# Gate and up of two FFNs by seven block products instead of eight

## The chip, the cores and the metric

The kernel runs on one core of a Trainium2 chip (trn2). Its time is the device time of one execution in microseconds (us). In the profile the engines are PE (TensorE, with PEld for its weight loads), DVE (VectorE), ACT (ScalarE), POOL (GpSimd) and SP (SyncE, which here only issues transfers). Each engine works off its own instructions in a fixed order; one that has to wait holds up all behind it on that engine.

## The reference

A diffusion backbone of two layers over 256 latent and 256 context tokens with 1024 features, all in float32. Each layer is a half FFN, a token mixer (grouped Fourier mixing in layer 0, bidirectional retention in layer 1), and a second half FFN:

```python
def half_ffn(t, m, j):
    h = modulate(rmsnorm(t, norm_g[l, j]), m[3 * j], m[3 * j + 1])
    return t + 0.5 * m[3 * j + 2] * swiglu(h, ffn_w_gate[l, j // 2], ffn_w_up[l, j // 2], ffn_w_down[l, j // 2])
def swiglu(h, w_gate, w_up, w_down):
    return (jax.nn.silu(h @ w_gate) * (h @ w_up)) @ w_down
```

The inner width is 2816. Both streams, latent and context, go through the same weights; only the last half FFN runs on the latent stream alone. The modulation vectors `m` (nine per layer, 1024 long, one set for each stream) come from products of a conditioning vector with 75 MB of weights.

## The kernel before

Activations lie transposed: features on the 128 partitions, in 8 tiles ("d tiles"), tokens in columns 0..255 (latent) and 256..511 (context). The four FFNs are called FFN 0 to 3 here (`f` in the code).

**Precision.** Float32 is reached by splitting each operand into two float32r parts, `hi` and `lo` (`split`: a cast on ScalarE for `hi`, a subtraction on VectorE for `lo`), and three matmuls for each product: hi x hi, hi x lo, lo x hi (`mm3`, lines 121 to 123 of the profile). So all weights pass through ScalarE (L88, tile `wh`) and VectorE (L89, tile `wl`) in tiles of 128 x 1024, after a transfer into `raw` (L95, queue of SP). `wpool` holds 5 such pairs, `rpool` 3 raw tiles of 2048 columns.

**An FFN** (`half_ffn`). The inner width is 22 tiles of 128 ("f tiles"), done in three chunks (`CHUNKS`: 8, 7, 7). For an f tile, gate and up are two PSUM tiles of 128 x 512 (both streams), each the sum over 8 d tiles of three matmuls: 48 matmuls of 512 columns, with two weight tiles of 1024 columns. `hidden` then makes silu(gate) on ScalarE (L383), the product with up on VectorE (L385), and its split, into `a` tiles. After each chunk the down projection adds into the residual (`residual`, L331); in the last chunk `project_last` finishes the latent half first, so that the norm of the next sublayer (`prepare`, `norm_mod`, L325 to L327) runs beside the context half.

**The head of FFN 1 and 2** (`begin_two`): two f tiles are done for the latent stream first, in matmuls of 256 columns, then the context's norm (`late`) and their context half. Their weights' `lo` parts are made on POOL.

**Modulation vectors** are worked ahead on VectorE (`pump`, `ada_step`, L211): a step is one d tile of one vector, for both streams, and reads 512 KB through POOL's queue (L202, two buffers `araw`). `pump(1.5)` follows each f tile and each of the four blocks of the down projection in FFN 1 and 2, with a credit for the halves, until all 128 steps are done.

**Order.** The program is written with a tile framework whose scheduler orders the instructions of each engine at build time; `tc.issue_after(x)` keeps a group behind instruction x.

Of the kernel before, what the change touches and what calls it, by code (L numbers as in the profile page):

```python
# [35 lines left out]
def hybrid_block(ctx: ExitStack, tc: tile.TileContext, a: dict, out: bass.AP):  # L36
    nc = tc.nc
    const = ctx.enter_context(tc.tile_pool(name="const", bufs=1))
    hpool = ctx.enter_context(tc.tile_pool(name="hpool", bufs=16))
# [57 lines left out]

    def wblock(src, n, other=None, lo_eng=None):
        """Loads up to 2048 columns, as pairs of parts that add up exactly, in tiles of 1024."""
        raw = load_raw(src, n)  # L100
        if other is not None:
            two = load_raw(other, n)
            for i, op in enumerate((ALU.add, ALU.subtract)):
                u, v = (t.rearrange("p (g f c) -> p g f c", f=2, c=256)[:, :, i] for t in (raw, two))
                nc.gpsimd.tensor_tensor(u, u, v, op)
# [988 lines left out]
```

## Time and profile before

| what | value |
|---|---|
| time, median of 3 runs (lowest, highest) | 1686.03 us (1685.74, 1686.68) |
| span of the profiled execution | 1685.4 us |
| busy: PE, DVE, ACT, POOL | 97%, 68%, 37%, 10% of the span |
| matmuls; instructions on DVE | 9384; 1769 |
| read from HBM | 261.08 MB, 156 GB/s over the span |
| share of the chain that ended last | PE 91%, DVE 5%, DMA 2%, ACT 1% |

The span is the time from the first to the last instruction of one profiled execution; the timed runs lie some 0.6 us above it. A duration in the profile is that of one instruction from start to end. Instructions of one engine overlap a little at their ends, so what an engine needs for a row of them is read from start to start in the timeline. A window (`A:B`) gives the busy time of each engine between two times, and the clock that TensorE was granted (PEclk, 1.00 is full).

### The profile page before, as it was taken

To read this page: it belongs to the slowest core of one execution; us is meant where nothing else is said; L and a number is where in the kernel's file an instruction comes from. 1 tells how busy PE (TensorE), PEld (TensorE's weight loads), DVE (VectorE), ACT (ScalarE), POOL (GpSimd) and SP (SyncE) were. 2 spreads that over 40 slices of the span, in tenths; PEclk is the share of its full clock that TensorE was granted. 3 is DMA by queue.
4 is the path that set the end of the run, shared out by engine and by line. 5 is a ranking of instruction groups with operands and counts; after the bars stand their busy time and mean duration, and the time that the engine had idled before them with its cause. 6 is when DMAs were issued, how large, how long until landed. Compare 5 with 4: busy or idle time off the path is not lost.

```text
span 1685.4 us, 23227 instructions
## 1 busy us (share of the span) xinstructions
PE 1637.7 (97%) x9384; PEld 1432.7 (85%) x9384; DVE 1142.5 (68%) x1769; ACT 624.0 (37%) x904; POOL 176.1 (10%) x213
## 2 busy tenths in 40 slices
PE   6999999997999999999999999999999999999998
PEld 4788888886888888888888888888998989999998
DVE  5678788768876766766567766743577657575554
ACT  4522322244452223223343132223465354454444
POOL 0011011035210000000400000000400000110000
PEclk9999999998999999999999999999999999999999
DMA  9555555554224554554234444522233324345452
GB/s 334 211 189 200 193 185 209 190 175 150 89 88 150 175 175 161 177 172 165 104 124 164 172 159 166 178 103 94 76 125 125 126 101 150 125 165 180 169 194 69
DMA packets 52892, 263.63 MB, mean 156 GB/s; under 512 B 6321, under 2 KB 7729, under 8 KB 34609
## 3 DMA queue, kind: packets, MB, share of 16 engines
q1 hardware_dynamic: 33664, 193.46, 32.7%
q0 software_dynamic: 18576, 68.17, 12.0%
q8 instruction: 73, 1.20, 0.3%
q10 hardware_dynamic: 544, 0.52, 0.1%
q14 instruction: 35, 0.28, 0.0%
HBM read 261.08 MB, written 1.05 MB: 156 GB/s over the span
## 4 chain that ended last, share of the span: by engine, by line
PE 91%; DVE 5%; DMA 2%; ACT 1%; issue 1%; SPq 0%; DVEq 0%; ACTq 0%
PE ps L122 30%; PE ps L121 30%; PE ps L123 30%; DMA a<-in_ada_first 1%; DVE q L325 1%; DVE h L327 1%; ACT wh L88 1%; DVE wl L89 1%; DVE q L286 0%; DMA xctx<-in_x 0%; PE ps L702 0%; DMA raw<-in_wgu 0%; DVE xctx L331 0%; PE aux L239 0%; DVE q L267 0%
## 5 line engine op out<-in xcount | busy, mean ns | idle before, releaser
L88 ACT CAST wh<-raw 128x1024 fp32r<-128x1024 f32 x344 | 353.2, 1030 | 714.7 <-PE ps L122 665.4
L122 PE MATMUL ps<-h,wh 128*128 128x512 f32 (+1 forms) x1600 | 564.2, 354 | 5.2 <-DVE h L327 5.2
L123 PE MATMUL ps<-h,wl 128*128 128x512 f32 (+1 forms) x1600 | 562.3, 354 | 0.0
L121 PE MATMUL ps<-h,wh 128*128 128x512 f32 (+1 forms) x1600 | 556.5, 355 | 3.7 <-ACT h L88 2.7
L89 DVE TENSOR_TENSOR wl<-raw,wh 128x1024 fp32r<-128x1024 f32 x328 | 392.6, 1199 | 172.6 <-ACT wh L88 163.6
L122 PEld LDWEIGHTS ps<-h,wh 128*128 128x128 f32 x1600 | 303.0, 189 | 48.2 <-DVE h L327 6.7
L121 PEld LDWEIGHTS ps<-h,wh 128*128 128x128 f32 x1600 | 299.4, 190 | 46.0 <-ACT h L88 3.5
L123 PEld LDWEIGHTS ps<-h,wl 128*128 128x128 f32 x1600 | 302.8, 189 | 41.2
L211 DVE CUSTOM_DVE_ANT_0 dump<-araw,wide,adab 128x1024 bf16<-128x1024 f32 x256 | 329.4, 1287 | 3.8
L122 PE MATMUL ps<-a,wh 128*128 128x256 f32 (+2 forms) x980 | 324.1, 332 | 0.0
L123 PE MATMUL ps<-a,wl 128*128 128x256 f32 (+2 forms) x980 | 323.6, 331 | 0.0
L121 PE MATMUL ps<-a,wh 128*128 128x256 f32 (+2 forms) x980 | 322.0, 331 | 0.0
L122 PEld LDWEIGHTS ps<-a,wh 128*128 128x128 f32 x980 | 186.1, 190 | 17.6
L123 PEld LDWEIGHTS ps<-a,wl 128*128 128x128 f32 x980 | 186.1, 190 | 17.4
L121 PEld LDWEIGHTS ps<-a,wh 128*128 128x128 f32 x980 | 185.2, 190 | 17.5
L385 DVE TENSOR_TENSOR t<-ps,t 128x512 f32<-128x512 f32 (+1 forms) x88 | 55.0, 625 | 189.9 <-PE ps L123 182.8
L202 POOL DMA_DIRECT2D araw<-in_ada_w x128 | 67.7, 529 | 809.4 <-DVE mods L211 742.4
L331 DVE SCALAR_TENSOR_TENSOR xlat<-ps,mods,xlat 128x256 f32<-128x256 f32 x128 | 61.1, 481 | 72.0 <-PE ps L123 71.4
L383 ACT ACTIVATE t<-ps 128x512 f32<-128x512 f32 (+1 forms) x88 | 47.9, 545 | 133.2 <-PE ps L123 133.2
L89 DVE TENSOR_TENSOR a<-t,a 128x512 fp32r<-128x512 f32 (+2 forms) x116 | 73.4, 637 | 3.9 <-ACT a L88 3.6
L89 POOL TENSOR_TENSOR wl<-raw,wh 128x1024 fp32r<-128x1024 f32 x16 | 40.1, 2522 | 312.3 <-ACT wh L88 312.3
L88 ACT CAST a<-t 128x512 fp32r<-128x512 f32 (+2 forms) x116 | 64.2, 557 | 9.2 <-DVE t L731 7.4
(189 smaller groups left out, 1200.9 us busy)
## 6 DMA issues: line engine op xcount, KB each, us to landing
raw<-in_wgu SPq DMA_DIRECT2D x85, 1024.0 KB, 5.0
araw<-in_ada_w POOLq DMA_DIRECT2D x128, 512.0 KB, 3.7
raw<-in_wd SPq DMA_DIRECT2D x32, 896.0 KB, 5.8
raw<-in_ret_in SPq DMA_DIRECT2D x24, 1024.0 KB, 4.8
raw<-in_wd SPq DMA_DIRECT2D x16, 1024.0 KB, 6.3
a<-in_ada_first SPq DMA_DIRECT2D x32, 256.0 KB, 5.2
raw<-in_four_w SPq DMA_DIRECT2D x8, 1024.0 KB, 4.8
raw<-in_ret_out SPq DMA_DIRECT2D x8, 1024.0 KB, 4.7
```

The source lines that it names most:

```text
L88: nc.scalar.copy(hi, src)
L89: i = (lo_eng or nc.vector).tensor_tensor(lo, src, f32(hi), ALU.subtract)
L121: nc.tensor.matmul(ps, lh, rh, start=start, stop=False)
L122: nc.tensor.matmul(ps, lh, rl, start=False, stop=False)
L123: mark[4] = nc.tensor.matmul(ps, ll, rh, start=False, stop=stop)
L202: nc.gpsimd.dma_start(raw, a["ada_w"][l, m, d])
L211: nc.vector.tensor_tensor_reduce(dump, raw, wide[:, v, :], 1.0, adab[:, l, m, d : d + 1], ALU.mult, ALU.add, mods[l][:, m, d, v : v + 1],)
L325: nc.vector.scalar_tensor_tensor(u, x_tile(d, s), sc, r, ALU.mult, ALU.mult)
L327: done.append(nc.vector.scalar_tensor_tensor(lo, u, sh, f32(hi), ALU.add, ALU.subtract))
L331: mark[0] = nc.vector.scalar_tensor_tensor(x_tile(d, s), ps, mods[l][:, m, d, s : s + 1], x_tile(d, s), ALU.mult, ALU.add)
L383: mark[1] = nc.scalar.activation(sg[:, :width], psg[:, :width], AF.Silu)
L385: nc.vector.tensor_tensor(hf[:, :width], psu[:, :width], sg[:, :width], ALU.mult)
```

## The change

For FFN 1 and FFN 2 the f tiles are taken in 11 pairs, and a pair's gate and up are computed by Strassen's method in Winograd's form: a block matrix product with blocks A11, A12 (first f tile, halves of d), A21, A22 (second f tile) and B11, B21 (latent stream, halves of d), B12, B22 (context stream). Seven products of blocks take the place of eight. Each product is 4 d tiles x gate and up x 3 matmuls of 256 columns, 24 in all, into one PSUM tile.

- **Activations** (`norm_blocks`, once per FFN): beside B11, B21 and B22 four blocks T1 to T4 of sums and differences of the streams' halves, each cast and split; 28 `h` tiles instead of 16.
- **Weights** (`pair_weights`, per pair): four sums S1 to S4 of 128 x 1024, made in place on the raw tiles by VectorE (L440 of the new file), and seven tiles to cast and split (L88 there) instead of four.
- **Results** (`pair_steps`): products accumulate in three PSUM tiles per pair; three are copied out by ScalarE (`kept`), three sums are made on VectorE (L495, L510, L517), and silu and the product with up go in four pieces of 256 columns (L478, L476).
- **Head** (`run_pairs`): two pairs are interleaved; their products with the latent stream come first, then the context's norm, then the rest. `begin_two`, and the `lo` parts on POOL with it, are no longer used by FFN 1 and 2. `pump` is called twice for the two pairs of the head, and twice for each pair after them.
- **Room**: chunks of 8, 8, 6 f tiles in all FFNs; raw tiles of 1024 columns (7 of them, so twice as many transfers of half the size); 4 weight pairs instead of 5; 18 `a` tiles instead of 22; some tiles of the Fourier mixing, retention and the first modulation move to `h` tiles; the scratch of POOL's transfers is set to 4096 bytes.

```diff
-CHUNKS = ((0, 8), (8, 15), (15, 22))
+CHUNKS = ((0, 8), (8, 16), (16, 22))
...
-    hpool = ctx.enter_context(tc.tile_pool(name="hpool", bufs=16))
-    apool = ctx.enter_context(tc.tile_pool(name="apool", bufs=22))
-    tpool = ctx.enter_context(tc.tile_pool(name="tpool", bufs=6))
+    hpool = ctx.enter_context(tc.tile_pool(name="hpool", bufs=28))
+    apool = ctx.enter_context(tc.tile_pool(name="apool", bufs=18))
+    tpool = ctx.enter_context(tc.tile_pool(name="tpool", bufs=8))
...
-    mpool = ctx.enter_context(tc.tile_pool(name="mpool", bufs=2))
-    rpool = ctx.enter_context(tc.tile_pool(name="rpool", bufs=3))
-    wpool = ctx.enter_context(tc.tile_pool(name="wpool", bufs=5))
+    rpool = ctx.enter_context(tc.tile_pool(name="rpool", bufs=7))
+    wpool = ctx.enter_context(tc.tile_pool(name="wpool", bufs=4))
...
     def load_raw(src, n):
-        raw = rpool.tile([P, 2048], F32, tag="raw", name=nm("raw"))
-        nc.sync.dma_start(raw[:, :n], src)
+        raw = []
+        for o in range(0, n, WT):
+            m = min(WT, n - o)
+            raw.append(rpool.tile([P, WT], F32, tag="raw", name=nm("raw")))
+            nc.sync.dma_start(raw[-1][:, :m], src[:, o : o + m])
         return raw
...
+    def blocks_of_h():
+        return {b: [(h_tile(), h_tile()) for _ in range(2)] for b in ("B11", "B21", "T1", "T2", "T3", "B22", "T4")}
+    def norm_blocks(l, j, s, H, r, V):
+        last = []
+        def values(i):
+            v = a_tile(F32)
+            with tc.issue_after(last[-2].ins) if len(last) > 1 else nullcontext():
+                for o in range(2):
+                    d = 2 * i + o
+                    u = q_tile()
+                    sc, sh = mods[l][:, 3 * j + 1, d, s : s + 1], mods[l][:, 3 * j, d, s : s + 1]
+                    nc.vector.scalar_tensor_tensor(u, x_tile(d, s), sc, r, ALU.mult, ALU.mult)
+                    nc.scalar.activation(v[:, o * S : o * S + S], u, AF.Identity, bias=sh)
+            return v
+        def parts(b, i, v):
+            hi, lo = H[b][i]
+            nc.scalar.copy(hi, v)
+            last.append(nc.vector.tensor_tensor(lo, v, f32(hi), ALU.subtract))
+        if s == 0:
+            for i in range(4):
+                V[i] = values(i)
+                parts(("B11", "B21")[i // 2], i % 2, V[i])
+        else:
+            n1, n2, v12, v22 = [], [], [], []
+            for i in range(2):
+                v12.append(values(i))
+                n1.append(t_tile())
+                nc.vector.tensor_tensor(n1[i], V[i], v12[i], ALU.subtract)
+                parts("T1", i, n1[i])
+            for i in range(2):
+                v22.append(values(2 + i))
+                n2.append(t_tile())
+                nc.vector.scalar_tensor_tensor(n2[i], n1[i], -1.0, v22[i], ALU.mult, ALU.subtract)
+                parts("T2", i, n2[i])
...
+            for i in range(2):
+                t = t_tile()
+                nc.vector.scalar_tensor_tensor(t, n2[i], -1.0, V[2 + i], ALU.mult, ALU.subtract)
+                parts("T4", i, t)
+        mark[0] = last[-1]
+    def pair_weights(f, p):
+        a11, a12 = load_raw(a["wgu"][f, 2 * p], 2048)
+        a21, a22 = load_raw(a["wgu"][f, 2 * p + 1], 2048)
+        at = {"A11": a11, "A12": a12, "A22": a22, "S1": a21, "S2": a11, "S3": a11, "S4": a12}
+        sums = [("S1", a21, a22, ALU.add), ("S2", a11, a21, ALU.add), ("S4", a12, a11, ALU.add), ("S3", a11, a22, ALU.subtract)]
+        def block(b):
+            while any(o == b for o, *_ in sums):
+                _, u, v, op = sums.pop(0)
+                nc.vector.tensor_tensor(u, u, v, op)
+            hi = wpool.tile([P, WT], F32R, tag="wh", name=nm("wh"))
+            lo = wpool.tile([P, WT], F32R, tag="wl", name=nm("wl"))
+            split(hi, lo, at[b])
+            return hi, lo
+        return block
+    def pair_steps(f, p, H, hid):
+        block = pair_weights(f, p)
+        al, be, ga = (ps_tile() for _ in range(3))
+        made, keep = {}, {}
+        def product(ps, w, b, first, ks=range(4)):
+            if 0 in ks:
+                made[w] = block(w)
+            wh, wl = made[w]
+            for k in ks:
+                hi, lo = (t[:, k % 2 * S : k % 2 * S + S] for t in H[b][k // 2])
+                for gu in range(2):
+                    o = gu * 512 + k * P
+                    for i, (u, v) in enumerate(((wh, hi), (wh, lo), (wl, hi))):
+                        mark[4] = nc.tensor.matmul(
+                            ps[:, gu * S : gu * S + S], u[:, o : o + P], v, start=(first and k + gu + i == 0),
+                            stop=(k == 3 and i == 2), skip_group_check=True,
+                        )
+        def kept(n, ps):
+            keep[n] = t_tile()
+            nc.scalar.copy(keep[n], ps)
+        def silu_mult(c, dst, sign=1.0):
+            g = q_tile()
+            mark[1] = nc.scalar.activation(g, c[:, :S], AF.Silu, scale=sign)
+            if sign < 0:
+                nc.vector.scalar_tensor_tensor(dst, c[:, S:], sign, g, ALU.mult, ALU.mult)
+            else:
+                nc.vector.tensor_tensor(dst, c[:, S:], g, ALU.mult)
+        at = len(hid)
+        hid += [(a_tile(), a_tile()) for _ in range(2)]
+        def out(n):
+            split(*hid[at + n], keep[n])
+        def p1(ks=range(4)):
+            product(al, "A11", "B11", True, ks)
+            if 3 in ks:
+                kept("p1", al)
+        def p2(ks=range(4)):
+            product(be, "A12", "B21", True, ks)
+            if 3 in ks:
+                c = t_tile()
+                nc.vector.tensor_tensor(c, be, keep["p1"], ALU.add)
+                keep[0] = t_tile()
+                silu_mult(c, keep[0][:, :S])
+        def p5():
+            product(ga, "S1", "T1", True)
+            kept("p5", ga)
+        def p6():
+            product(al, "S2", "T2", False)
+            kept("u2", al)
+        def p7():
+            product(al, "S3", "T3", False)
+            c = t_tile()
+            nc.vector.scalar_tensor_tensor(c, al, -1.0, keep["p5"], ALU.mult, ALU.subtract)
+            keep[1] = t_tile()
+            silu_mult(c, keep[1][:, S:])
...
+        def p4():
+            product(al, "A22", "T4", False)
+            silu_mult(al, keep[1][:, :S], -1.0)
+            out(1)
+        return p1, p2, p5, p6, p7, p3, p4
...
+            if paired:
+                run_pairs(f, h, hid, c0 // 2, c1 // 2)
+                i = c1
+            elif c0 == 0:
...
+    def prepare(l, j, width, paired=False):
...
+                norm = (lambda s, r: norm_blocks(l, j, s, h, r, V)) if paired else (lambda s, r: norm_mod(l, j, s, h, r))
+                norm(0, rstd(0))
...
+    def run_pairs(f, H, hid, p0, p1):
+        if p0 == 0:
+            two = [pair_steps(f, p, H, hid) for p in range(2)]
+            for n in range(2):
+                for ks in ((0, 1), (2, 3)):
+                    for steps in two:
+                        steps[n](ks)
+                if n == 0:
+                    nxt["late"](0)
+            nxt["late"](1)
+            for n in range(2, 7):
+                for steps in two:
+                    steps[n]()
+                if n == 4:
+                    pump(RATE[f])
+            pump(RATE[f])
+            p0 = 2
+        for p in range(p0, p1):
+            s1, s2, s5, s6, s7, s3, s4 = pair_steps(f, p, H, hid)
+            for n, step in enumerate((s1, s2, s6, s5, s7, s3, s4)):
+                step()
+                if n == 4:
+                    pump(RATE[f])
+            pump(RATE[f])
...
-    fourier(0, 0, nxt["h"], late, prepare(0, 2, T2))
-    half_ffn(0, 2, nxt["h"], T2, begin_two, prepare(1, 0, T2))
+    fourier(0, 0, nxt["h"], late, prepare(0, 2, T2, True))
+    half_ffn(0, 2, nxt["h"], T2, begin_two, prepare(1, 0, T2, True))
...
-    nc = bacc.Bacc("TRN2", target_bir_lowering=False, num_devices=1)
+    nc = bacc.Bacc("TRN2", target_bir_lowering=False, num_devices=1, dynamic_dma_scratch_size=4096)
```

Three places show how the instructions stand before and after. In all of them `xctx` is the context's residual, `raw` a weight tile as loaded, `wh` and `wl` its parts, `h` an activation's parts, `ps` a PSUM tile, `dump` a half step of the modulation vectors.

VectorE at the head of FFN 1, before: the context's norm begins (reciprocal, then one scaling and one `lo` part per d tile).

```order
L286 RECIPROCAL q_872_4229<-q_871_4227 128x256
L325 SCALAR_TENSOR_TENSOR q_873_4282<-xctx_1_94,mods0_123,q_872_4229 128x256
L325 SCALAR_TENSOR_TENSOR q_874_4286<-xctx_1_94,mods0_123,q_872_4229 128x256
L325 SCALAR_TENSOR_TENSOR q_875_4290<-xctx_1_94,mods0_123,q_872_4229 128x256
L327 SCALAR_TENSOR_TENSOR h_823_4077<-q_873_4282,mods0_123,h_822_4076 128x256
L325 SCALAR_TENSOR_TENSOR q_876_4294<-xctx_1_94,mods0_123,q_872_4229 128x256
L327 SCALAR_TENSOR_TENSOR h_825_4079<-q_874_4286,mods0_123,h_824_4078 128x256
```

VectorE there, after; `raw_924` to `raw_927` are the second pair's weights, `ps_918` and `ps_929` hold the second products of the two pairs.

```order
L440 TENSOR_TENSOR raw_926_4264<-raw_926_4264,raw_927_4266 128x1024
L495 TENSOR_TENSOR t_948_4385<-ps_918_4254,t_939_4319 128x512
L440 TENSOR_TENSOR raw_924_4260<-raw_924_4260,raw_926_4264 128x1024
L88 TENSOR_TENSOR wl_978_4506<-raw_926_4264,wh_977_4505 128x1024
L440 TENSOR_TENSOR raw_925_4262<-raw_925_4262,raw_924_4260 128x1024
L88 TENSOR_TENSOR wl_981_4537<-raw_913_4245,wh_980_4536 128x1024
L478 TENSOR_TENSOR t_949_4387<-t_948_4385,q_950_4388 128x256
L495 TENSOR_TENSOR t_951_4403<-ps_929_4269,t_940_4333 128x512
L88 TENSOR_TENSOR wl_984_4568<-raw_924_4260,wh_983_4567 128x1024
L440 TENSOR_TENSOR raw_913_4245<-raw_913_4245,raw_916_4251 128x1024
L393 SCALAR_TENSOR_TENSOR q_955_4410<-xctx_1_91,mods0_120,q_943_4339 128x256
```

The reciprocal and the context's scalings stood together; now these weight sums, weight splits and two sums out of PSUM stand between them.

TensorE at the same place, before: the end of the latent half of the second f tile, then the context half (`h_822` is the first d tile's `hi` part).

```order
L121 MATMUL ps_864_4169<-h_836_4090,wh_868_4176 128x256
L122 MATMUL ps_864_4169<-h_837_4091,wh_868_4176 128x256
L123 MATMUL ps_864_4169<-h_836_4090,wl_869_4177 128x256
L121 MATMUL ps_861_4166<-h_822_4076,wh_857_4158 128x256
L121 MATMUL ps_862_4167<-h_822_4076,wh_857_4158 128x256
L121 MATMUL ps_863_4168<-h_822_4076,wh_866_4172 128x256
```

TensorE there, after: the end of the second pair's product with B21, then S1 times T1 (`h_871` and `h_872` are the `hi` and `lo` part of T1's first two d tiles; `ps_919` belongs to the first pair, `ps_930` to the second).

```order
L463 MATMUL ps_929_4269<-h_869_4155,wh_946_4357 128x256
L463 MATMUL ps_929_4269<-h_870_4156,wh_946_4357 128x256
L463 MATMUL ps_929_4269<-h_869_4155,wl_947_4358 128x256
L463 MATMUL ps_919_4255<-h_871_4157,wh_974_4474 128x256
L463 MATMUL ps_930_4270<-h_871_4157,wh_977_4505 128x256
L463 MATMUL ps_919_4255<-h_872_4158,wh_974_4474 128x256
```

What follows the latent products now reads T1, a difference of latent and context values, and S1, a sum of weights; before it read the context's normalised values themselves.

VectorE in the middle of FFN 1, before: from one f tile's product of gate and up to the next one's.

```order
L385 TENSOR_TENSOR t_959_4797<-ps_957_4746,t_958_4795 128x512
L89 TENSOR_TENSOR wl_994_4962<-raw_992_4959,wh_993_4961 128x1024
L89 TENSOR_TENSOR a_961_4800<-t_959_4797,a_960_4799 128x512
L211 ISA dump_962_4803,mods1_124<-araw_947_4727,wide_122,adab_107 128x1024
L211 ISA mods1_124 128x1
L211 ISA dump_963_4805,mods1_124<-araw_947_4727,wide_122,adab_107 128x1024
L211 ISA mods1_124 128x1
L89 TENSOR_TENSOR wl_996_4966<-raw_992_4959,wh_995_4965 128x1024
L385 TENSOR_TENSOR t_973_4871<-ps_971_4820,t_972_4869 128x512
```

VectorE in the middle of the second chunk of FFN 1, after: from the split of one pair's S3 (`raw_1253`) to the sum that follows its product; `raw_1299` to `raw_1302` belong to the next pair.

```order
L88 TENSOR_TENSOR wl_1279_6321<-raw_1253_6177,wh_1278_6320 128x1024
L214 ISA dump_1247_6165,mods1_121<-araw_1206_5912,wide_119,adab_104 128x1024
L214 ISA mods1_121 128x1
L88 TENSOR_TENSOR wl_1287_6361<-raw_1254_6179,wh_1286_6360 128x1024
L88 TENSOR_TENSOR wl_1291_6396<-raw_1256_6183,wh_1290_6395 128x1024
L88 TENSOR_TENSOR wl_1311_6456<-raw_1299_6440,wh_1310_6455 128x1024
L214 ISA dump_1248_6167,mods1_121<-araw_1206_5912,wide_119,adab_104 128x1024
L214 ISA mods1_121 128x1
L440 TENSOR_TENSOR raw_1299_6440<-raw_1299_6440,raw_1301_6444 128x1024
L510 SCALAR_TENSOR_TENSOR t_1280_6348<-ps_1257_6185,t_1277_6316 128x512
L214 ISA dump_1250_6171,mods1_121<-araw_1239_6095,wide_119,adab_104 128x1024
L214 ISA mods1_121 128x1
```

Two weight splits and a step stood between two results out of PSUM; now, between S3's split and the sum behind its product, stand three more weight splits, a weight sum and a step.

More of the change, by code (lines that the diff above doesn't have):

```diff
@@ L78, in a_tile, with h_tile @@
         return apool.tile([P, 512], dt, tag="a", name=nm("a"))
-    def h_tile():
-        return hpool.tile([P, 512], F32R, tag="h", name=nm("h"))
+    def h_tile(dt=F32R):
+        return hpool.tile([P, 512], dt, tag="h", name=nm("h"))
     def f32(ap):
@@ L101, in wblock @@
         if other is not None:
[L102 to L105, printed above, removed]
+            for pair in zip(raw, load_raw(other, n)):
+                for i, op in enumerate((ALU.add, ALU.subtract)):
+                    u, v = (t.rearrange("p (g f c) -> p g f c", f=2, c=256)[:, :, i] for t in pair)
+                    nc.gpsimd.tensor_tensor(u, u, v, op)
         pairs = []
-        for o in range(0, n, WT):
+        for o, t in zip(range(0, n, WT), raw):
             m = min(WT, n - o)
@@ L110, in wblock @@
             lo = wpool.tile([P, WT], F32R, tag="wl", name=nm("wl"))
-            split(hi[:, :m], lo[:, :m], raw[:, o : o + m], lo_eng)
+            split(hi[:, :m], lo[:, :m], t[:, :m], lo_eng)
             pairs.append((hi, lo))
@@ L372, in project_last @@
         after(1)
+    def blocks_of_h():
[34 more added lines that the diff above has]
+                t = t_tile()
+                nc.vector.tensor_tensor(t, v22[i], v12[i], ALU.subtract)
+                parts("T3", i, t)
+            for i in range(2):
+                parts("B22", i, v22[i])
+            for i in range(2):
+                t = t_tile()
+                nc.vector.scalar_tensor_tensor(t, n2[i], -1.0, V[2 + i], ALU.mult, ALU.subtract)
+                parts("T4", i, t)
+        mark[0] = last[-1]
@@ new lines, in pair_steps, with p3 @@
+    def pair_steps(f, p, H, hid):
[52 more added lines that the diff above has]
+            silu_mult(c, keep[1][:, S:])
+        def p3():
+            product(ga, "S4", "B22", False)
+            c = t_tile()
+            nc.vector.tensor_tensor(c, ga, keep["u2"], ALU.add)
+            silu_mult(c, keep[0][:, S:])
+            out(0)
+        def p4():
[3 more added lines that the diff above has]
+        return p1, p2, p5, p6, p7, p3, p4
@@ L375, in half_ffn @@
     def half_ffn(l, j, h, width, begin, after, each=None):
+        paired = isinstance(h, dict)
         f = 2 * l + j // 2
@@ L444, in fourier @@
         raw = load_raw(a["dft"][:, :1280], 1280)
-        dft = [(a_tile(), a_tile()) for _ in range(2)]
+        dft = [(h_tile(), h_tile()) for _ in range(2)]
         for i, (hi, lo) in enumerate(dft):
-            split(hi, lo, raw[:, 512 * i : 512 * i + 512], nc.gpsimd)
+            split(hi, lo, raw[0][:, 512 * i : 512 * i + 512], nc.gpsimd)
         fix = a_tile()[0:33, :S]
-        nc.scalar.copy(fix, raw[0:33, 1024:1280])
+        nc.scalar.copy(fix, raw[1][0:33, :256])
         def dcols(o):
             return tuple(t[:, o % 512 : o % 512 + S] for t in dft[o // 512])
-        tails = mpool.tile([P, 512], F32, tag="mk", name="tails")
+        tails = h_tile(F32)
         nc.sync.dma_start(tails, a["dft"][:, 1280:1792])
@@ L461, in fourier @@
         nc.scalar.mul(edge, ident[:64].unsqueeze(1).broadcast_to([64, 2, P]), 0.0)
-        even = [(a_tile(), a_tile()) for _ in range(4)]
+        even = [(a_tile(), h_tile()) for _ in range(4)]
         odd = [(a_tile(), a_tile()) for _ in range(2)]
@@ L619, in masks @@
             nc.vector.scalar_tensor_tensor(m2, delta, 0.0, e2, ALU.is_le, ALU.mult)
-            own = mpool.tile([P, 512], F32, tag="mk", name=nm("mk"))
+            own = h_tile(F32)
             nc.vector.tensor_tensor(own, m1, m2, ALU.add)
@@ L869, in late @@
                     else:
-                        norm_mod(l, j, 1, h, nxt["r"])
+                        norm(1, nxt["r"])
                 nxt["late"] = late
```

16 lines of the change are left out of this document (7 added, 9 removed).

## The prediction

> **What bounds the kernel now.** I read the page's busy line and the chain of waits first, then windows over FFN 1 and FFN 2, then the timeline of TensorE and VectorE inside them.
>
> ```profile
> PE 1637.7 (97%) x9384; PEld 1432.7 (85%) x9384; DVE 1142.5 (68%) x1769; ACT 624.0 (37%) x904; POOL 176.1 (10%) x213
> ...
> PE 91%; DVE 5%; DMA 2%; ACT 1%; issue 1%; SPq 0%; DVEq 0%; ACTq 0%
> ```
>
> TensorE is the bound nearly everywhere: 97% busy, 91% of the chain. The two changed FFNs begin with the scalings of their latent norm and the reciprocal before them:
>
> ```profile
> 471.91 1.26 DVE L325 SCALAR_TENSOR_TENSOR q<-xlat,mods,aux 128x256 f32<-128x256 f32 x3 [2.21 <-PE aux L311]
> ...
> 831.98 1.75 DVE L286 RECIPROCAL q<-q 128x256 f32<-128x256 f32 x1 [2.37 <-ACT q L283]
> ...
> 1196.95 1.75 DVE L286 RECIPROCAL q<-q 128x256 f32<-128x256 f32 x1 [2.37 <-ACT q L283]
> ```
>
> So FFN 1 takes 472 to 832, 360 us, and FFN 2 takes 832 to 1197, 365 us. Windows over both (columns: PE, PEld, DVE, ACT, POOL busy with counts, clock, DMA share, GB/s):
>
> ```profile
> 472.00:832.00 360.00, 359.57 (x1738) 304.50 (x1738) 243.01 (x359) 109.18 (x146) 37.04 (x58) 1.00 0.45 155
> 832.00:1197.00 365.00, 363.36 (x1771) 307.66 (x1770) 226.01 (x323) 111.73 (x151) 36.99 (x49) 1.00 0.41 140
> ```
>
> TensorE never stops there. VectorE has 117 and 139 us left, and the question is whether the new sums fit. Prices per instruction, read from start to start:
>
> ```profile
> 540.25 0.39 PE L121 MATMUL ps<-h,wh 128*128 128x512 f32 x1
> ...
> 558.61 0.39 PE L121 MATMUL ps<-h,wh 128*128 128x512 f32 x1
> ...
> 483.91 0.28 PE L121 MATMUL ps<-h,wh 128*128 128x256 f32 x1
> ...
> 484.63 0.28 PE L121 MATMUL ps<-h,wh 128*128 128x256 f32 x1
> ...
> 542.72 1.23 DVE L89 TENSOR_TENSOR wl<-raw,wh 128x1024 fp32r<-128x1024 f32 x1
> 543.86 0.68 DVE L89 TENSOR_TENSOR a<-t,a 128x512 fp32r<-128x512 f32 x1
> 544.46 1.28 DVE L211 CUSTOM_DVE_ANT_0 dump<-araw,wide,adab 128x1024 bf16<-128x1024 f32 x1
> ...
> 547.12 1.28 DVE L211 CUSTOM_DVE_ANT_0 dump<-araw,wide,adab 128x1024 bf16<-128x1024 f32 x1
> ...
> 447.48 0.41 DVE L551 TENSOR_TENSOR t<-ps,t 128x256 f32<-128x256 f32 x1
> 447.81 0.41 DVE L552 TENSOR_TENSOR t<-ps,t 128x256 f32<-128x256 f32 x1
> 448.14 0.47 DVE L331 SCALAR_TENSOR_TENSOR xlat<-t,mods,xlat 128x256 f32<-128x256 f32 x1
> 448.53 0.47 DVE L331 SCALAR_TENSOR_TENSOR xctx<-t,mods,xctx 128x256 f32<-128x256 f32 x1
> ```
>
> Between the first two rows lie 81 matmuls: 18.36 / 81 = 0.227 us for 512 columns. Between the next two lie 6: 0.72 / 6 = 0.120 us for 256, more than half. On VectorE 1024 columns cost 1.14, 512 cost 0.60, 256 cost 0.33 or, with a scalar operand, 0.40, and a modulation step (two halves, 544.46 to 547.12) 2.66 us. To see that such prices add up, I multiplied them with the instructions that FFN 1 and 2 had before: 240 and 217 us. The windows show 243 and 226 busy, the rest being stretched instructions at the heads (below).
>
> **TensorE's part of the change.** A pair before is 96 matmuls of 512 columns, 96 x 0.227 = 21.8 us; after, 168 of 256, 168 x 0.120 = 20.2. The two f tiles of the head were in 256 columns already, 192 x 0.120 = 23.0. Per FFN: 23.0 + 10 x 21.8 = 240.7 before, 11 x 20.2 = 221.8 after, so 18.9 less, 37.8 for both. That is all the change can gain on TensorE. The smaller last chunk changes nothing worth counting.
>
> **VectorE's part.** A pair before: 4 weight splits (4.6), two products of gate and up and their splits (4 x 0.60 = 2.4), three modulation steps (8.0), together 15.0 beside 21.8 of TensorE. After: 7 weight splits and 4 weight sums (11 x 1.14 = 12.5), three sums out of PSUM and two splits (3.0), four products of 256 (1.5), the same three steps (8.0), together 25.0 beside 20.2. The in-place sum has no row before; I price it as the split, the same operation on the same sizes. It could be as dear as a half step (1.33) or, from below, nothing dearer than the 0.60 of 512 columns if some faster form applied: 43 sums in an FFN then shift it by +8 or -23 us of VectorE time; no row shows a faster form, so 1.14. With 14 splits and 8 sums of activations (512 columns) in each norm, in place of 16 `lo` parts, VectorE needs 361 us for FFN 1 and 335 for FFN 2 by all its instructions. FFN 1 alone thus fills VectorE for as long as the whole of it takes now. FFN 2 is lighter since the 128 steps run out in it.
>
> What counts is where it lies. While gate and up run, VectorE needs 22 to 24 us from one pair to the next by the new order (two to four steps moved into the down projection), over TensorE's 20.2; in the down projections TensorE needs more. Stage by stage, the larger of the two, FFN 1 first.
>
> *Head, to the second block of the third pair.* Two waits, both for rooms and data that the first weights hold:
>
> ```profile
> L88 ACT CAST wh<-raw 128x1024 fp32r<-128x1024 f32 x344 | 353.2, 1030 | 714.7 <-PE ps L122 665.4
> ...
> raw<-in_wgu SPq DMA_DIRECT2D x85, 1024.0 KB, 5.0
> ```
>
> The fifth weight tile (S1) needs a `wpool` buffer from the first product: about 7 us after the first scaling, plus a cast of 1.03 and a split, 9.2. The eighth raw tile of the two pairs needs the buffer that this split frees (seven buffers), so it lands at 14.2 (5.0 from issue; half the size may take less). Behind it on VectorE stand four weight sums, three splits and two sums out of PSUM (9.5), and only then the context's scalings, and T1 (4.9): T1 is there at 28.6. TensorE had four products, 11.5 us from 2.7 on, and waits from 14.2 to 28.8. Then 12 products, 34.6, and 2.5 for a clock that has dropped by then: 66 us. VectorE's own sum ends at 64. Before, the same wait was nothing.
>
> ```profile
> 398.00:404.00 6.00, 3.26 (x13) 2.89 (x14) 5.94 (x14) 3.84 (x10) 2.66 (x3) 0.58 0.50 175
> 404.00:410.00 6.00, 6.00 (x27) 5.02 (x27) 5.97 (x10) 3.28 (x9) 4.04 (x3) 0.57 0.17 41
> ...
> 838.00:842.00 4.00, 3.13 (x24) 2.92 (x24) 4.00 (x6) 1.74 (x5) 2.68 (x1) 1.00 0.04 14
> ```
>
> After a real stop (398 to 404) the clock stood near half for some 5 us, half of which is the 2.5; with TensorE idle in crumbs (838 to 842, 78% busy) it stayed at 1.00. [...]
>
> *The rest of FFN 1.* Pairs 3 and 4: VectorE 45.5; its last 4 (the tail of the last result) lie beside the next stage, 41.5. Down projection, 192 x 0.227 = 43.5, with two products of the next pair, 5.8: 49.3 on TensorE (VectorE 41.8). Four pairs of chunk 2: 90.8 - 4 = 86.8 on VectorE (TensorE 74.9). Down: 49.3. Three pairs: 65.9 - 4 = 61.9 (TensorE 54.7). Last down to the next reciprocal: 72 x 0.227 + 72 x 0.120 = 25, and 2 for the norm's sum and root. Together 66 + 41.5 + 49.3 + 86.8 + 49.3 + 61.9 + 27 = 382, against 360: +22.
>
> *FFN 2* begins at its reciprocal, so its head is 72; then 38.8, 49.3, 87.4, 49.3; with no steps left the last three pairs are TensorE's, 54.7, and 27: 378.5 against 365, +13.5.
>
> *POOL's splits go.* They had stretched VectorE's instructions:
>
> ```profile
> 838.58 2.68 POOL L89 TENSOR_TENSOR wl<-raw,wh 128x1024 fp32r<-128x1024 f32 x1 [2.24 <-ACT wh L88]
> ...
> 833.96 3.46 DVE L325 SCALAR_TENSOR_TENSOR q<-xlat,mods,q 128x256 f32<-128x256 f32 x3
> ...
> 838.92 2.62 DVE L325 SCALAR_TENSOR_TENSOR q<-xlat,mods,q 128x256 f32<-128x256 f32 x1
> ```
>
> Three scalings took 3.46 instead of 1.3 and one 2.62 instead of 0.48, some 4.3 us in FFN 2's head. Since the stages above use undisturbed prices, this gain is in them. [...]
>
> *The rest.* Seven weight splits and sums (8.0) move into the end of the Fourier mixing, where VectorE is on the chain; they fill gaps and what POOL no longer takes: +2 (0 to 8). ScalarE per pair: seven casts, three copies, silu and casts, some 11 us of 22: hidden by VectorE's queue, and if it is late VectorE waits; with SP's and POOL's transfers I put all waits inside VectorE's stretches (455 us) at 2%, +8 (0 to 20), as 404 to 410 shows VectorE at 5.97 of 6 when it is the bound. Twice as many transfers on SP's queue, fewer weight and `a` buffers elsewhere, and POOL's smaller scratch cost 0 as long as ScalarE's casts wait for TensorE (665 of 715 us of their idle time, above); if that cover goes in retention or FFN 3, a few us. I take 0 (0 to +6).
>
> Sum: 1685.4 + 22 + 13.5 + 2 + 8 = 1731, on the profiled execution's span, which lies 0.6 below the median of the runs; that changes nothing at this size.
>
> **Rivals.** (a) *Slower modulation.* TensorE sets the time after all, since steps yield: without them VectorE needs 17 us per pair, under 20.2. It decides where fewer than 1.2 steps stand between two pairs; the order has two to three, and VectorE cannot pass over them. If it held, and the heads' stops with it (2 x 12), the time is 1686 - 38 + 24 = 1672; without those stops 1648. [...] (c) *Balance*: VectorE runs ahead in the down projections so far that the stops of both FFNs cost no more than the 38 saved, 1686. The four weight buffers hold less than one pair, so hardly. (d) *The products don't get cheaper*: with weight loads of 190 ns not overlapped, 168 x 0.19 = 31.9 a pair, 22 x 10 = 220 more, 1906; the 0.120 of the rows above, with a new weight tile each, speaks against it.
>
> **How the numbers follow.** The forecast (1700 to 1755) gets 0.66, (a) 0.11, (b) and more waits of that size 0.17, (c) 0.03, (d) 0.01, and 0.02 lies between (c) and the forecast. Time 1731. The range takes the forecast with its costs' ends and most of (b): 1698 to 1772. Faster by over 0.2% (3.4 us, about what a measurement of this kernel can tell from no change): 0.11; within: 0.03; slower: 0.86.
>
> **What the profile after would show.** VectorE over 90% busy in pairs and TensorE's idle time before L463 put down to VectorE's L88 (`wl`); a stop of 12 to 16 us ahead of S1 x T1 in both FFNs, with a clock near 0.5 behind it; 0.120 us per matmul inside a product; VectorE's `raw` sums at 1.14; FFN 1 longer by more than FFN 2. I am wrong if TensorE stays above 97% in FFN 1, if the sums cost far less than 1.14, or if the heads have no stop.

## The result, and the profile after

The changed kernel takes 1721.61 us (median of 3, 1721.04 to 1727.68): 1.0225 times the kernel before, 95% interval 1.0211 to 1.0239. Its profiled span is 1719.2, 33.8 more than before. The head of its page:

```profile
PE 1611.7 (94%) x10740; PEld 1475.5 (86%) x10740; DVE 1363.6 (79%) x2053; ACT 743.6 (43%) x1108; POOL 163.3 (9%) x213
...
PE 83%; DVE 10%; DMA 2%; issue 2%; ACT 2%; POOL 1%; SPq 0%; DVEq 0%; ACTq 0%; POOLq 0%
...
L440 DVE TENSOR_TENSOR raw<-raw,raw 128x1024 f32<-128x1024 f32 x88 | 107.3, 1219 | 9.7 <-DMA raw<-in_wgu 9.4
```

TensorE is busy 26 us less and its share of the chain falls from 91 to 83%. VectorE has 221 us more, about half of it the 88 weight sums. VectorE's timeline dates the stages, by the reciprocal of each latent norm:

```profile
396.05 1.74 DVE L289 RECIPROCAL q<-q 128x256 f32<-128x256 f32 x1
...
479.58 0.17 DVE L306 RECIPROCAL inv<-root 128x2 f32<-128x2 f32 x1 [2.25 <-ACT root L302]
...
854.65 1.74 DVE L289 RECIPROCAL q<-q 128x256 f32<-128x256 f32 x1
...
1227.79 1.75 DVE L289 RECIPROCAL q<-q 128x256 f32<-128x256 f32 x1 [1.07 <-ACT q L286]
```

With the same rows of before (388.73, 469.01, 831.98, 1196.95) and of each experiment's trace, in us:

| kernel | to the end of FFN 0 | Fourier mixing | FFN 1 | FFN 2 | rest | time / before (95%) |
|---|---|---|---|---|---|---|
| before | 388.7 | 80.3 | 363.0 | 365.0 | 488.5 | 1 |
| after | 396.1 | 83.5 | 375.1 | 373.1 | 491.4 | 1.0225 (1.0211-1.0239) |
| rooms | 399.0 | 81.1 | 364.8 | 371.7 | 491.8 | 1.0116 (1.0100-1.0132) |
| nosum | 397.9 | 80.9 | 360.8 | 362.8 | 491.8 | 1.0023 (1.0013-1.0033) |
| entry2 | 390.1 | 103.3 | 375.8 | 373.0 | 492.1 | 1.0284 (1.0263-1.0304) |
| head3 | 396.5 | 78.9 | 381.2 | 380.2 | 494.1 | 1.0267 (1.0250-1.0284) |
| steps | 396.9 | 81.7 | 370.7 | 376.5 | 489.2 | 1.0174 (1.0159-1.0189) |
| entry3 | 393.1 | 83.9 | 374.4 | 373.1 | 492.0 | 1.0181 (1.0161-1.0201) |
| warm | 398.6 | 83.3 | 375.9 | 372.1 | 492.7 | 1.0210 (1.0191-1.0229) |
| best | 393.7 | 84.3 | 370.4 | 375.2 | 491.6 | 1.0185 (1.0163-1.0207) |
| poolsplit | 395.4 | 84.8 | 378.8 | 374.8 | 491.0 | 1.0238 (1.0223-1.0253) |
| poolsum | 396.2 | 86.6 | 400.2 | 390.9 | 492.8 | 1.0480 (1.0462-1.0497) |
| rooms2 | 391.7 | 81.6 | 364.8 | 371.9 | 492.7 | 1.0094 (1.0077-1.0111) |
| light | 395.1 | 81.8 | 358.4 | 361.8 | 493.5 | 1.0023 (1.0014-1.0033) |

The stages come from one profiled execution each; the median of before was 1686 to 1690 on the chips of the experiments, so single stages compare to about a us, and whole times by the ratio. Rooms, nosum, entry2 and head3 ran on one chip, steps to best on a second, poolsplit and poolsum on a third, the last two on a fourth.

Of the 33.8, only 20.3 lie in FFN 1 and 2. In the head of FFN 1, VectorE, then TensorE, then two windows behind the stop (columns as in the prediction):

```profile
496.00 1.23 DVE L440 TENSOR_TENSOR raw<-raw,raw 128x1024 f32<-128x1024 f32 x1 [1.78 <-DMA raw<-in_wgu]
...
504.35 1.22 DVE L440 TENSOR_TENSOR raw<-raw,raw 128x1024 f32<-128x1024 f32 x1
505.48 1.67 DVE L393 SCALAR_TENSOR_TENSOR q<-xctx,mods,q 128x256 f32<-128x256 f32 x4
```

```profile
496.01 0.40 PE L463 MATMUL ps<-h,wh 128*128 128x256 f32 x2
...
497.33 0.28 PE L463 MATMUL ps<-h,wl 128*128 128x256 f32 x1
509.93 1.30 PE L463 MATMUL ps<-h,wh 128*128 128x256 f32 x3 [12.32 <-ACT h L399]
...
515.48 0.27 PE L463 MATMUL ps<-h,wl 128*128 128x256 f32 x1
```

```profile
510.00:516.00 6.00, 6.00 (x29) 5.78 (x30) 6.00 (x12) 4.83 (x10) 0.00 (x0) 0.55 0.00 0
516.00:522.00 6.00, 6.00 (x52) 6.00 (x52) 6.00 (x10) 5.67 (x9) 0.00 (x0) 1.00 0.00 0
```

The context's scalings (505.48) stand behind four sums of weights. The first, the second pair's S1, waits for its load; the other three (S2, S4, S3) are for products that come later than S1 x T1. TensorE stops for 12.3 us, and then 29 matmuls run in 6 us instead of 52: another 2.6. From 496.01 to 497.33 start 11 matmuls, 0.120 each, so a pair's 168 need 20.2, and the chunks of 4, 4 and 3 pairs 80.6, 80.6 and 60.5. TensorE's timeline gives their gate and up in FFN 1 as 98.4, 86.4 and 62.7, in all 247.5 where the eight products took 242.5. So the chunk with the head loses 17.8 and the other seven pairs 8.0.

FFN 1 ends and FFN 2 begins like this on TensorE (the reciprocal above, at 854.65, comes with the last product; before, it came 5 us ahead of it):

```profile
854.87 0.28 PE L126 MATMUL ps<-a,wl 128*128 128x256 f32 x1
861.26 0.80 PE L463 MATMUL ps<-h,wh 128*128 128x256 f32 x2 [6.11 <-ACT h L399]
```

Outside the FFNs, what TensorE waits for from the end of FFN 0 to FFN 1's norm, before and after:

```profile
PE ps L123 <- DVE h L327: 6.7, 4, 2.4
PE ps L121 <- ACT t L88: 3.2, 3, 1.2
PE aux L295 <- DVE q L267: 2.9, 1, 2.9
```

```profile
PE ps L124 <- ACT h L87: 17.5, 1, 17.5
PE aux L298 <- DVE q L270: 10.0, 1, 10.0
PE ps L125 <- POOL h L88: 1.6, 1, 1.6
```

The first new wait is for the split of the transform's matrix, the second for the squares ahead of FFN 1's norm, which stand behind splits and sums of FFN 1's weights on VectorE.

The end of FFN 0 is 7.3 us later. Ahead of the mixing's norm POOL adds up squares (L267 before, L270 after); before, its last one waits for ScalarE alone, after, the last two wait behind sums of the Fourier weights. Before and after:

```profile
386.27 0.74 POOL L267 TENSOR_TENSOR q<-q,q 128x256 f32<-128x256 f32 x1 [0.96 <-ACT q L260]
```

```profile
388.34 3.54 POOL L108 TENSOR_TENSOR raw<-raw,raw 128x512 f32<-128x512 f32 x2
391.84 2.39 POOL L270 TENSOR_TENSOR q<-q,q 128x256 f32<-128x256 f32 x2
```

### The profile page after: what moved, and what is told of

It is laid out like the page before. It is cut to its first block, busy times and chain, and to the rows that moved or that the text cites. A ratio compares the mean times of both kernels' runs of the same rounds, so it can differ in the third digit from the quotient of the medians.

```text
span 1719.2 us, 26940 instructions
## 1 busy us (share of the span) xinstructions
PE 1611.7 (94%) x10740; PEld 1475.5 (86%) x10740; DVE 1363.6 (79%) x2053; ACT 743.6 (43%) x1108; POOL 163.3 (9%) x213
## 4 chain that ended last, share of the span: by engine, by line
PE 83%; DVE 10%; DMA 2%; issue 2%; ACT 2%; POOL 1%; SPq 0%; DVEq 0%; ACTq 0%; POOLq 0%
PE ps L463 21%; PE ps L125 20%; PE ps L124 20%; PE ps L126 20%; DVE wl L88 2%; DVE raw L440 2%; DVE dump L214 1%; ACT wh L87 1%; DMA raw<-in_four_w 1%; POOL raw L108 1%; DVE q L328 1%; DMA raw<-in_wgu 1%; DVE a L88 0%; DVE h L330 0%; DMA xctx<-in_x 0%
## 5 line engine op out<-in xcount | busy, mean ns | idle before, releaser
L87 ACT CAST wh<-raw 128x1024 fp32r<-128x1024 f32 (+1 forms) x410 | 418.9, 1033 | 622.3 <-PE ps L125 378.8
L88 DVE TENSOR_TENSOR wl<-raw,wh 128x1024 fp32r<-128x1024 f32 (+1 forms) x402 | 483.5, 1209 | 142.1 <-ACT wh L87 137.0
L463 PE MATMUL ps<-h,wh 128*128 128x256 f32 x2464 | 456.1, 288 | 38.3 <-ACT h L399 31.1
L463 PE MATMUL ps<-h,wl 128*128 128x256 f32 x1232 | 347.0, 287 | 1.4 <-DVE wl L88 1.4
L124 PE MATMUL ps<-a,wh 128*128 128x512 f32 (+2 forms) x968 | 317.5, 333 | 3.2 <-ACT wh L87 3.2
L126 PE MATMUL ps<-a,wl 128*128 128x256 f32 (+1 forms) x968 | 319.3, 333 | 0.0
L125 PE MATMUL ps<-a,wh 128*128 128x256 f32 (+1 forms) x936 | 312.1, 335 | 0.0
L125 PE MATMUL ps<-h,wh 128*128 128x512 f32 (+2 forms) x864 | 290.1, 336 | 5.7 <-DVE h L330 5.5
L124 PE MATMUL ps<-h,wh 128*128 128x512 f32 (+1 forms) x832 | 278.3, 339 | 4.6 <-ACT h L87 2.7
L126 PE MATMUL ps<-h,wl 128*128 128x512 f32 (+1 forms) x832 | 280.2, 338 | 0.0
L126 PEld LDWEIGHTS ps<-a,wl 128*128 128x128 f32 x968 | 183.4, 190 | 17.8
L125 PEld LDWEIGHTS ps<-a,wh 128*128 128x128 f32 x936 | 177.7, 190 | 17.8
L440 DVE TENSOR_TENSOR raw<-raw,raw 128x1024 f32<-128x1024 f32 x88 | 107.3, 1219 | 9.7 <-DMA raw<-in_wgu 9.4
```

The costliest lines, as they stand in the source:

```text
L87: nc.scalar.copy(hi, src)
L88: i = (lo_eng or nc.vector).tensor_tensor(lo, src, f32(hi), ALU.subtract)
L124: nc.tensor.matmul(ps, lh, rh, start=start, stop=False)
L125: nc.tensor.matmul(ps, lh, rl, start=False, stop=False)
L126: mark[4] = nc.tensor.matmul(ps, ll, rh, start=False, stop=stop)
L440: nc.vector.tensor_tensor(u, u, v, op)
```

## Experiments

**rooms.** `prepare(0, 2, T2, True)` and `prepare(1, 0, T2, True)` lose their `True`: eight products in the changed kernel's rooms.

> The changed kernel with gate and up of FFN 1 and FFN 2 by eight products again, as before; its rooms, its 1024-column loads, its chunks of 8, 8 and 6 f tiles and its POOL scratch stay. Theory A (VectorE's added sums and splits inside the two FFNs cost the time; rooms and loading cost only what the start of the Fourier mixing shows): FFN 1 360 and FFN 2 365 us as before, the stretch ahead of FFN 1's norm still about 10 longer, retention about 3 longer; 1698 us in all (1694 to 1703). Rival B (rooms and loading cost the FFNs too): over 1710. Rival B0 (rooms cost nothing, all of it is the products): 1686.

Half of the loss is there without a single product changed: 1.0116. Only 2 us of it fall to FFN 1; the end of FFN 0 costs 10.3 (7.3 in after), the rest 3.3 (2.9), and FFN 2 6.7, in its own head: its scalings lie beside four splits of POOL in a row (843.53 to 853.27), and TensorE waits 4.06 for one. The four weight buffers are the likely reason; no run changes them alone. That part is not in after, which has no POOL splits there, so the two halves don't simply add. A's 1698 is 8 short of this (1.0116 x 1686 = 1706), B (over 1710) overstates it, since FFN 1 is hardly touched, and by B0 the rooms would be free, which they are not.

**nosum.**

```diff
-                nc.vector.tensor_tensor(u, u, v, op)
```

> The changed kernel without the four weight sums of a pair: the seven products take the raw tiles as they are, so the sums are left out of the computation; splits, products and rooms stay. VectorE loses 44 x 1.14 = 50 us in each of the two FFNs. Theory A (VectorE bounds the pairs): FFN 1 375 to about 357, FFN 2 373 to about 357, 1687 us in all (1678 to 1697). Rival C (TensorE's clock, weight loads or the waits for rooms bound them): within 6 us of 1721.

1.0023 against 1.0225: without the sums 34 us less by the ratio, 27 by the stages (14.3 in FFN 1, 10.4 in FFN 2, 2.6 ahead of them). A stands by its numbers, C falls. Against rooms, which has the same rooms and all eight products, nosum is only some 16 us less (1.0116 to 1.0023): of the 37.8 that seven products save TensorE, more than half is lost even without the sums. A chunk of four pairs in windows, after:

```profile
626.60:712.00 85.40, 81.63 (x654) 80.35 (x654) 84.32 (x113) 41.44 (x59) 5.28 (x10) 0.98 0.49 156
```

and here:

```profile
616.60:700.00 83.40, 81.99 (x663) 80.62 (x662) 74.85 (x106) 42.95 (x60) 5.80 (x11) 1.00 0.55 172
```

VectorE is full in after (84.3 of 85.4) and loses 9.5 here, but the chunk, 86.4 with its last products among the down projection's, only becomes 83.4. The head gains most, 98.4 to 92.1: its stop falls from 12.3 to 6.7.

**entry2 and entry3.** Both load and split the transform's matrix ahead of the norm. In entry3 `nxt["sq0"]` is the last square on POOL ahead of the mixing, and the condition leaves out the first block of weights (the diff). In entry2 the line is `with tc.issue_after(nxt["sq"].ins):` for all four blocks, and `nxt["sq"]` is the last square on POOL so far: from the second block on, that is a square of the next norm, made from the output of the block before.

```diff
-                    nc.gpsimd.tensor_tensor(u, u, v, op)
+                    with tc.issue_after(nxt["sq0"].ins) if nxt["b"] else nullcontext():
+                        nc.gpsimd.tensor_tensor(u, u, v, op)
```

> The changed kernel with another order at the start of the Fourier mixing alone: the transform's matrix is loaded and split ahead of the norm, and POOL's sums of the Fourier weights stand behind its squares. Theory (POOL's queue and the late split of the matrix stop TensorE for 17 us there): 6 to 12 us less, 1712. Rival (the four weight splits that VectorE now does ahead of the norm are the cause): within 3 us of 1721.

> The changed kernel with the transform's matrix loaded and split ahead of the norm, as in entry2, but POOL's sums of the first block of Fourier weights stay where they were; only those of blocks 2 to 4 stand behind the squares ahead of the mixing. Theory B (in the changed kernel the sums of the later blocks, waiting for their loads, hold up POOL's squares and the split): the end of FFN 0 7 us earlier as in entry2, the mixing 80 instead of 83.5, 1711 us in all (1707 to 1715). Rival (the sums are needed as early as they stood, and holding back any of them costs the mixing what the norm gains): 1719 or more.

Entry2 ends FFN 0 7.8 earlier than nosum on the same chip, so POOL's queue was what held the norm; but the mixing becomes 20 longer. The first block's sums still run early (400.27), while those of the second stand behind such a square on POOL:

```profile
438.43 0.72 POOL L271 TENSOR_TENSOR q<-q,q 128x256 f32<-128x256 f32 x1 [32.58 <-ACT q L264]
439.11 5.95 POOL L109 TENSOR_TENSOR raw<-raw,raw 128x512 f32<-128x512 f32 x4
```

So each later block waits for the one before it, and TensorE for its weights, 24.2 us in three pieces. Entry3 ties those sums to the squares ahead of the mixing and gains 1.0225 to 1.0181, some 7 us, between its theory and the rival; in its trace FFN 0 ends 4 to 5 us ahead of steps and warm (396.9, 398.6), but the mixing is no shorter (83.9): the wait of 17.5 is gone, and four of 1.5 to 4.2 us in its place and the one of 10 at the end remain.

**rooms2**: rooms with entry3's edit.

> The kernel of rooms (eight products, the changed kernel's rooms and loading) with the order of entry3 at the start of the Fourier mixing. Theory B (half of what the rooms cost, 20 us, is POOL's and ScalarE's order there): 8 to 12 us less than rooms, 1.005 to 1.007 of before. Rival (the order costs only the 4 to 5 us that entry3 regained in the changed kernel, the rest is rooms proper: four weight buffers in FFN 2's head, h rooms in retention): 1.008 to 1.010.

The rival: 1.0094, though its interval overlaps that of rooms. The order at the mixing is a fifth of the rooms' cost by the ratio, a third by the stages (7.3 at the end of FFN 0); the rest lies in FFN 2's head (6.9, in that kernel alone), some 4 behind FFN 2 (retention and FFN 3), 3 at the end of FFN 0, and 1 to 2 each in the mixing and FFN 1. Which of the rooms cost that in retention was not tried.

**head3.** T1 ahead of the sums, S3 and S4 behind T2, eight raw buffers.

```diff
...
-                nc.vector.tensor_tensor(u, u, v, op)
+                with tc.issue_after(nxt["t1" if o in ("S1", "S2") else "t2"].ins):
+                    nc.vector.tensor_tensor(u, u, v, op)
```

> The changed kernel with another head of FFN 1 and FFN 2: VectorE makes T1 ahead of the weight sums of the first two pairs, S3 and S4 behind T2, and there are eight raw buffers (and 8 instead of 12 q tiles), so that the eighth tile waits for nothing. Theory A1 (the stop is an idle VectorE waiting for T1's place in the queue and for the room; VectorE idles 7 us there): 4 to 6 us less per head, 1711 in all. Rival A2 (the head is bound by the sum of VectorE's work, the stop only moves): 1717 to 1722. Rival: the smaller q pool costs more elsewhere than it gains: over 1725.

Slower than after: 1.0267, some 1731. By the number that is the third rival, the smaller q pool; the trace has what A2 says as well. What TensorE waits for in FFN 1, after and here:

```profile
PE ps L463 <- ACT h L399: 12.7, 2, 12.3
PE ps L463 <- ACT wh L87: 3.8, 3, 1.6
```

```profile
PE ps L468 <- ACT wh L87: 12.5, 5, 8.4
PE ps L468 <- DVE wl L88: 4.5, 4, 1.5
```

T1 is no longer waited for, S1 is. S1 x T1 begins 23.4 behind the first scaling, 4.0 earlier than in after, but the third pair begins 6.6 later than there (65.4 against 58.8): the stop only moves, since the sums had used time in which VectorE had nothing else. The same shows ahead of the norm, where the mixing falls to 78.9 with the sums gone from there, and FFN 1 pays it back. How much of the 6 to 7 an FFN comes from the smaller q pool is open, so this run alone doesn't show A2.

**steps.** RATE 2.4, 0.6, 0.6, 0.6; a rate of its own for the down blocks (2.4, 2.5, 2.5); no `pump` in the heads.

> The changed kernel with the modulation steps elsewhere: none in the heads, 1.2 instead of 3 between two pairs, 2.4 instead of 2 per f tile and per down block of FFN 0, 2.5 instead of 1.5 per down block of FFN 1 and 2. The same 128 steps are done. Theory A (VectorE's total work beside the pairs is the bound, whatever part of it): FFN 1 375 to about 362, FFN 2 373 to about 365, FFN 0 unchanged, 1700 us in all (1692 to 1710). Rival A3 (it is the order sum, split, product that costs, not the load): within 6 us of 1721. Rival: FFN 0 becomes bound by VectorE or by the steps' transfers: FFN 0 longer by 5 or more.

1.0174, 8 to 9 us less by the ratio: 1715.4, outside A's range and at the edge of A3's. The stages show 4.4 of it in FFN 1, where the trace has 31 steps in place of 42 (29 us less for VectorE), and 4 in the mixing and the rest, against 3.4 more in FFN 2; the load counts, but with little leverage. FFN 0 didn't mind.

**warm.** `keep_warm(40, mark[4])` behind the head's fourth product.

> The changed kernel with 40 idle products of TensorE behind the fourth product of the head in FFN 1 and FFN 2, where it stops for 13 us. Theory C (the clock that drops in the stop costs about 2.5 us a head): 4 to 6 us less, 1716. Rival (the stop's end and VectorE set the pace behind it anyway, so that a full clock only brings the next wait earlier): within 2 us of 1721.

Rival: 1.0210, no difference that the intervals show. TensorE's first products after the filled stop:

```profile
512.39 0.51 PE L463 MATMUL ps<-h,wh 128*128 128x256 f32 x2 [3.54 <-ACT h L399]
...
514.04 0.63 PE L463 MATMUL ps<-h,wh 128*128 128x256 f32 x2
514.46 0.41 PE L463 MATMUL ps<-h,wl 128*128 128x256 f32 x1
514.68 0.63 PE L463 MATMUL ps<-h,wh 128*128 128x256 f32 x2
```

The filling ended 3.54 us too early, and three matmuls still took 0.64 instead of 0.36 (clock 0.70 from 512.4 to 518). So this run does not price a clock that is held; it shows that 3.5 us idle cost about 1.8 us by the clock, where 12.3 cost 2.6.

**poolsplit.** The splits of A11 and A12 of the head's pairs get `nc.gpsimd`, as the first blocks before.

> The changed kernel with the first two weight splits of each of the first two pairs of FFN 1 and FFN 2 back on POOL, where the kernel before had them. Theory A2 (in the head the sum of VectorE's work sets when T1 and its weights are there): VectorE loses 4 x 1.14 = 4.6 us a head; less what POOL's instructions stretch it by (4.3 us a head in the kernel before), 0 to 4 less a head, 1713 to 1721 in all, and a shorter stop. Rival (POOL's splits, 2.7 us instead of 1.14, come too late for the first products, or hold VectorE up by more): 1723 or more.

1.0238, some 1726: in the rival's range, though its interval overlaps that of after. The stop is 12.3 again, so 4.6 us less of VectorE's splits did not shorten it; in FFN 1 they lie ahead of the norm (459.98 to 474.60) and not in it.

**poolsum.** `nc.gpsimd` for `nc.vector` in all sums.

> The changed kernel with all weight sums of the pairs on POOL. Theory (VectorE and POOL disturb each other, as in the head of the kernel before: 2.5 us per sum of 1024 columns on POOL, and VectorE's instructions stretched by about as much as they gain): 44 x 1.14 = 50 us leave VectorE in each FFN and most of it comes back by stretching: 1715 to 1735. Rival (POOL's idle time is free): as with the sums left out, 1690 to 1697. Rival (sums of 2.5 us in the chain of load, sum, cast, split, product make it longer than VectorE's load was): over 1740.

1.048: the last rival by its number, the first theory by what the trace shows. POOL, then VectorE at the same time:

```profile
650.01 2.40 POOL L440 TENSOR_TENSOR raw<-raw,raw 128x1024 f32<-128x1024 f32 x1 [1.07 <-DMA raw<-in_wgu]
```

```profile
650.35 3.15 DVE L88 TENSOR_TENSOR wl<-raw,wh 128x1024 fp32r<-128x1024 f32 x1
...
656.17 1.21 DVE L88 TENSOR_TENSOR wl<-raw,wh 128x1024 fp32r<-128x1024 f32 x1
```

A split of 1.21 takes 3.15 beside a sum. VectorE is busy 372 us in FFN 1, against 306 with the sums left out: POOL's 44 sums cost VectorE 66, more than the 50 that it saved. The stretched split ends 1.09 behind POOL's sum (650.35 + 3.15 against 652.41), nearly the 1.14 that one takes alone; beside the next two sums the splits of 1024 columns took 3.10 and 2.82 and ended 1.09 and 1.08 behind them. So in these three VectorE's work came as late as if it had begun where POOL's ended.

**best**: steps, entry3 and warm together. **light**: nosum, steps and entry3.

> The three edits of steps, entry3 and warm together. If they add up: 1721 - 21 - 10 - 5 = 1685, level with the kernel before (0.996 to 1.004 of it). If VectorE is no longer the bound in the pairs, the heads' edits gain more than alone: below 0.996. If the parts hide one another: over 1.004.

> The edits of nosum, steps and entry3 together: seven products without the weight sums (left out of the computation), 1.2 modulation steps between pairs, the matrix early. It asks what seven products could win here at most, with 50 us of sums and some 30 us of steps taken off VectorE in each FFN. If VectorE's load is what holds them: FFN 1 and FFN 2 at 350 each, 1670 us, 0.99 of before. If the stop in the heads and the rooms hold them: as nosum with what entry3 gains, 1686 to 1690, 1.000 to 1.002.

Best is no better than steps alone (1.0185): the parts hide one another, and no version here beats the kernel before. Light is level with nosum at 1.0023, some 1690, its second theory (heads and rooms); four pairs run in 81.9 there, 1.6% over TensorE's need, but TensorE still waits 16.7 us for activations at the two heads. So with VectorE at 283 us in FFN 1 instead of 355, FFN 1 and 2 gain 4.6 and 3.2 on before, and the stages around them take it.

## Why the prediction was right, and where only by luck

The sign held, and so did the mechanism: VectorE's added work, above all in the heads, costs more than TensorE saves. 1731 came out 10 too high. That it wasn't further off is luck: FFN 1 and 2 with their waits were forecast 23 us too dear, and the rest, put at nothing, took 10.

- *TensorE's gain, 18.9 an FFN*: held, 0.120 a matmul. *The sums at 1.14*: held (start to start 1.13 to 1.14, 1.219 each in the group).
- *The head*: held, nearly to the us. From the first scaling (482.55) TensorE stops at 15.1 and T1 releases it at 27.4 (forecast 14.2 and 28.8); the third pair's second product is through at 64.6 (forecast 66); 2.6 for the clock (forecast 2.5). Whether order or the sum of VectorE's work causes the stop is not settled: nosum shortens it to 6.7, and head3 speaks for the sum, but head3 has a smaller q pool too, and in poolsplit less work left the stop as it was.
- *Pairs at VectorE's pace, "22 to 24 us from one pair to the next"*: the step that failed. From the end of the head to the third product of chunk 1 took 85.0 (41.5 + 49.3 = 90.8 forecast), chunk 1 with its down projection, to the same product of chunk 2, 130.9 (136.1). VectorE was as full as forecast, but it worked ahead in the down projections by more than the 4 us I gave it: in the first one (585 to 626) stand four weight sums of the next pairs. 16 sums fewer a chunk, 18 us of VectorE's work, gained 3.0 us. *Waits at 2%, +8*: nothing was left for them.
- *The first two products of the next pair*, which I placed in each down projection, aren't there: the trace has the last two or three products of the pairs before in their place.
- *The end of FFN 1, 61.9 + 27 = 88.9*: 91.6. I let the reciprocal come 6 us ahead of the last product, as before; now it comes at 854.65, the last product at 854.87. Two splits and a sum of FFN 2's first weights stand ahead of it on VectorE (850.85 to 854.25), and FFN 2 begins with a stop of 6.1. FFN 1 and 2 together: +20.3, forecast 35.5 and the 8.
- *Sums at the end of the mixing, +2 (0 to 8)*: about 3 to 5 (83.5 against 80.9 in nosum and 78.9 in head3; waits of 10.0 there, 5.8 in rooms). In its range.
- *The rest, 0 (0 to +6)*: mis-sized. 7.3 at the end of FFN 0 and 3.0 behind FFN 2 alone. I named ScalarE's waiting for TensorE as the cover for buffers and queues, and looked at retention; at the mixing that cover isn't there, and POOL's sums, cut in halves and loaded early, stepped ahead of the squares.
- *POOL's splits go*: the 4.3 us a head that I counted for it is not shown; poolsplit, which puts four splits a head back on POOL, can't be told from after.

Of the rivals, (a) falls with light: even without sums the heads' stops remain. (b), the clock falling inside the pairs, sets the upper end of the range (1772) and has a chance of 0.17; no run shows what it would need, a fall behind every pair. In after the clock fell inside the pairs once in each of the two FFNs, to 0.50 for 3.4 us (682.67 to 686.08 and 1061.54 to 1064.97), which cost some 1.5 us each (last section). (c) falls with the time, (d) with the 0.120. Of what the profile was to show, VectorE over 90% busy, the stop, 0.55 of clock, 1.14 and FFN 1 the longer (12.1 against 8.2) are there, and TensorE is busy 95% of FFN 1; but in the pairs its idle time is put down to ScalarE's `wh` (3.8 in 3) more than to `wl` (0.9).

## What to carry to other kernels

Seven products instead of eight can pay up to 18.9 us an FFN here, and that only where the engine that makes the eighth's sums has time at the right place: price the head, where sums, norm and first splits meet, apart from the pairs, which an engine working ahead can carry at 99% busy. Price the rooms that the change needs as an edit of their own, by building the old work in the new rooms: here that was half of the loss. An edit that takes a visible stop away (head3, entry2, warm) often only hands it to the next thing in line.

## What the runs showed of the hardware

A stop of 3.5 us (warm) cost TensorE's clock much of what one of 12.3 (after) did, about 1.8 and 2.6 us, which I hadn't expected. The clock also fell behind a still shorter one, of 1.64 us, in the middle of the pairs of after (FFN 1; the 0.50 of the window is the clock):

```profile
682.00 1.14 PE L463 MATMUL ps<-h,wh 128*128 128x256 f32 x4 [1.64 <-ACT wh L87]
```

```profile
682.67:686.08 3.41, 3.41 (x17) 3.41 (x17) 3.41 (x5) 0.00 (x0) 0.00 (x0) 0.50 0.69 197
```

What the prediction calls a real stop in before (398 to 404) is made of short pieces too: up to 398.96, where the clock fell, the longest was 2.0 us (ahead of 396.73), and behind that one the clock was still 1.00 (396 to 398). So these runs don't give a length of stop from which the clock falls.

POOL's sums cost VectorE more (66 us in FFN 1 of poolsum) than they saved it (50): work handed to another engine saves no time where it stretches what stays, here a split from 1.21 to 3.15 us.
